# S5's state turned back on VectorE and GpSimd before the read-out, and the scale of x moved to the context's stage

## The chip, the cores and the metric

The kernel runs on one core of a Trainium2 chip. The time is device microseconds (us) of that core for one execution. TensorE does the matrix products, VectorE and ScalarE the element-wise work, GpSimd almost nothing, and SyncE's queue starts the DMA transfers.

## What is computed

Two blocks run one after the other on a sequence of 256 tokens of width 2048, in fp32. The first mixes an S5 branch and a gated delta-rule branch, and closes with a convolved feed-forward. The second modulates its input by vectors computed from a condition, then runs windowed attention beside a two-way RWKV recurrence over a context of 256 tokens and over x, then a feed-forward. Cut to what the change touches:

```
# S5, 64 groups of 16 channels, 64 complex states each
_, _, xr, xi = lax.associative_scan(combine, (ar_t, ai_t, bu_re, bu_im), axis=1)
y = (jnp.einsum("ghp,blgp->blgh", c_re.astype(f32), xr)
     - jnp.einsum("ghp,blgp->blgh", c_im.astype(f32), xi))
...
mod = jax.nn.silu(c) @ ada_w + ada_b                    # 2048 -> 6 x 2048
sh1, sc1, g1, sh2, sc2, g2 = jnp.split(mod[:, None, :], 6, axis=-1)
...
z  = modulate(rmsnorm_2(x,  norm1_g), sh1,  sc1)  @ w_in     # x * (1 + scale) + shift
zc = modulate(rmsnorm_2(xc, norm1_g), sh1c, sc1c) @ w_in
...
x = x + g1 * (jnp.concatenate([attn, rw], axis=-1) @ w_out)
x = x + g2 * swiglu(modulate(rmsnorm_2(x, norm2_g), sh2, sc2), ffn_w1, ffn_w3, ffn_w2)
```

## The kernel before

Data lies feature by feature: a tile is 128 features by 256 tokens. A scheduler (`tile.TileContext` with a timeline of its own) fixes the order of the instructions on every engine when the program is built; on the chip each engine works through its own list in order, and so does each DMA queue.

**Dense products** (`dense`, from L273). A weight is loaded in pieces of 256 by 512 (SyncE's queue), copied to a rounded high part on ScalarE (L269), and the low part is formed by a subtraction on VectorE (L270, called the weight split below). TensorE then does three products a piece (L298, L299, L301).

**The ada vectors.** The modulation is 2048 x 12288 weights, read once in 384 tiles of 128x512, and it is spread over the whole program. `ada_tick` takes one tile out of the list `self.ada`. `dense` calls it `tick_rate` times a weight piece: 0.72 at first, 0.2 in the context's path, 0.55 in the context's quads and the first feed-forward, 0.43 in the part of x, 0.5 in the second feed-forward. `ada_rows(n0, n1)` does 4 x (n1 - n0) tiles for the features n0 to n1 (in units of 128): for each quarter TensorE first spreads a piece of the condition over the partitions (`ada_c`, L235, a PSUM bank with the tag "ada" and one buffer), then each tile is loaded by SyncE's queue (L184, three buffers) and multiplied and summed by one VectorE instruction (L242). At the end two VectorE instructions write `mod` (L246, L247). Rows 0 to 16 are the shift of x, 16 to 32 its scale, 32 to 48 the gate, 48 to 64 and 64 to 80 the shift and scale of the second feed-forward, 80 to 96 its gate. `ada_start` sets the list for the first block, `ada_next` sets the one for the second when the first block is nearly through (after `w_out1`), and `ada_end` empties whatever is left of the list at once. `program` calls `ada_end` before `attention`.

**S5** (`s5_setup` from L826, `s5` from L912). The recurrence runs in a turning frame: two products bring the input into the states, VectorE turns them by cosine and sine, two scans run per state half, and VectorE multiplies the result V (real part V[0], imaginary part V[1]) by the cosine (P1) and the sine (P2). That gives four arrays of 128x256. The turned-back state is (P1[0] - P2[1], P1[1] + P2[0]); the read-out takes the four arrays separately, with the matrices CP[0], CP[1] = -CP[0], CN and CN, and lets PSUM add them (L958 to L960). 64 groups in pairs make 32 rounds of this, in 16 pairs of rounds.

**Attention** (`attention` from L1634). For each of 4 key heads and 2 query blocks: scores (L1667, L1670), softmax, transposes (L1683), the output products (`at_po`, L1689), and a spread of the sums' reciprocals into the same tile (L1702). The tile of `at_po` has the PSUM tag "ada" too, with one buffer. The scheduler lays the RWKV quads of x beside it: scores (L1352), a block inversion (L627 to L642) and a chain of four steps (L1433 to L1462) for each quad.

Of the kernel before, what the change touches and what calls it, by code (L numbers as in the profile page):

```python
# [14 lines left out]
ALU = mybir.AluOpType  # L15
# [74 lines left out]
class Kern:  # L90
# [87 lines left out]
    def ada_start(self):  # L178

        self.ada = itertools.chain(self.ada_rows(16, 32, 1), self.ada_cols(), self.ada_rows(16, 32))  # L180
# [37 lines left out]
    def ada_next(self):  # L218
        self.ada_end()
        self.ada = itertools.chain(self.ada_rows(32, 64), self.ada_rows(64, 80))  # L220
# [605 lines left out]
    def s5_setup(self):  # L826
        nc = self.nc
        v = nc.vector
# [40 lines left out]
        kr, ki = t("kr"), t("ki")  # L869
# [9 lines left out]
        cT = [self.tq([128, 32, 32], name=f"s5_c{w}") for w in range(2)]  # L879
        for w in range(2):  # L880
            nc.sync.dma_start(cT[w], self.a["s5_cT"][:, w])
        CP = [self.tq([128, 32, 32], name=f"s5_cp{w}") for w in range(2)]
        CN = self.tq([128, 32, 32], name="s5_cn")
        tm = self.tq([128, 32, 32], name="s5_ct")
        bk = lambda ap: ap.unsqueeze(2).to_broadcast([128, 32, 32])
        v.tensor_tensor(tm, cT[1], bk(ki), ALU.mult)
        v.tensor_tensor(CP[0], cT[0], bk(kr), ALU.mult)
        v.tensor_tensor(CP[1], tm, CP[0], ALU.subtract)
        v.tensor_tensor(CP[0], CP[0], tm, ALU.subtract)
# [22 lines left out]
    def s5(self):  # L912
# [6 lines left out]
        for i8 in range(8):  # L919
# [3 lines left out]
            for q0 in (0, 2):  # L923
# [18 lines left out]
                for e in range(2):  # L942
# [14 lines left out]
                    Q.append((P1[:, 0], P2[:, 1], P1[:, 1], P2[:, 0]))  # L957
                for k, C in enumerate((self.CP[0], self.CP[1], self.CN, self.CN)):  # L958
                    for e in range(2):
                        nc.tensor.matmul(py[rows[e]], lhsT=C[:, i + e], rhs=Q[e][k], start=k == 0, stop=k == 3)  # L960
# [216 lines left out]
    def mod1(self):  # L1177

        self.gs1 = self.tiny([128, 2, 16], name="gs1")
        for w in range(2):  # L1180
            self.nc.vector.scalar_tensor_tensor(self.gs1[:, w], self.mod[:, w, 16:32], 1.0, self.P("norm1_g"), ALU.add,
                                                ALU.mult)

        fw = self.P("final_norm_w")
        self.gfw, self.w2e = self.tiny([128, 16], name="gfw"), self.tiny([128, 16], name="w2e")
        self.nc.vector.tensor_tensor(self.gfw, self.gs1[:, 0], fw, ALU.mult)
        self.nc.vector.tensor_tensor(self.w2e, fw, fw, ALU.mult)
        self.nc.vector.tensor_scalar(self.w2e, self.w2e, EPS, None, ALU.add)
# [596 lines left out]
    def program(self, out):  # L1785
# [24 lines left out]
        self.tick_rate = 0.43  # L1810
        self.mid_norms()
# [122 lines left out]
```

## Time and profile before

| what | value |
|---|---|
| runs | 3480.36, 3486.3 and 3485.99 us, median 3485.99 |
| the profiled execution: its own time, its span | 3484.27 us, 3482.5 us |
| mean granted clock of TensorE | 0.975 of full speed |
| busy: TensorE, VectorE, ScalarE, GpSimd | 96%, 72%, 44%, under 1% |
| S5 beside dense products | 383 to 731 us |
| the 64 tiles of the scale of x | 592 to 893 us |
| second block's first 192 ada tiles | 893 to 2327 us |
| attention beside RWKV quads | 2345 to 2524 us |

The busy share is an average over stages with different limits. A stretch shows its own limit: the engine that is busy nearly all of the stretch sets the pace there. Where no engine is, they wait for each other, and the waits tell which step ends last. The granted clock says at which of its two levels TensorE ran.

### The profile page before, as it was taken

What the parts mean: (1) busy time and instruction counts of PE and PEld (TensorE: products, weight loads), DVE (VectorE), ACT (ScalarE), POOL (GpSimd) and SP (SyncE); (2) the same over time, 40 slices, a digit from 0 to 9 for tenths busy, and PEclk for the clock granted to TensorE, in tenths of its full rate; (3) what the DMA queues carried; (4) which work ended last, traced back from release to release, by engine and by line L of the source; (5) the groups of instructions that cost most, each with busy time, mean ns of one, the idle gap of its engine ahead of it and who ended that gap; (6) DMA issues with size and microseconds to landing.
All of it is one profiled execution on the core that took longest, in us unless ns stands there. A gap on an engine that the chain in (4) does not pass through costs nothing. (4 is left out here: it accounts for less than half of the span.)

```text
span 3482.5 us, 72752 instructions
## 1 busy us (share of the span) xinstructions
PE 3341.5 (96%) x30680; PEld 3073.5 (88%) x30680; DVE 2506.8 (72%) x4245; ACT 1515.8 (44%) x2148; POOL 17.0 (0%) x46
## 2 busy tenths in 40 slices
PE   8999999999999999999999999998898999999998
PEld 7889767898998889999999988886686999999997
DVE  7787777877668878967777778686666666665556
ACT  5434334444454444434444454443433443333433
POOL 0000000000000000000000000000000000000000
PEclk9999999999998999999999999997899999999999
DMA  7655555667654445456676664450123676655554
GB/s 234 184 167 172 179 173 183 190 217 254 209 176 158 139 160 165 157 192 225 227 230 219 223 198 148 141 174 2 33 98 100 211 226 225 228 188 182 182 187 146
DMA packets 337287, 618.37 MB, mean 178 GB/s; under 512 B 25184, under 2 KB 49504, under 8 KB 336960
## 3 DMA queue, kind: packets, MB, share of 16 engines
q1 hardware_dynamic: 336736, 612.66, 54.7%
q8 instruction: 240, 3.93, 0.5%
q0 software_dynamic: 224, 1.07, 0.1%
q14 instruction: 87, 0.71, 0.1%
HBM read 608.39 MB, written 4.72 MB: 176 GB/s over the span
## 5 line engine op out<-in xcount | busy, mean ns | idle before, releaser
L270 DVE TENSOR_TENSOR wl<-w,wr 128x1024 fp32r<-128x1024 f32 (+2 forms) x928 | 1110.5, 1197 | 654.2 <-ACT wr L269 619.8
L269 ACT CAST wr<-w 128x1024 fp32r<-128x1024 f32 (+2 forms) x928 | 953.3, 1028 | 1382.6 <-PE acc L299 1172.0
L298 PE MATMUL acc<-hh,wr 128*128 128x256 f32 (+2 forms) x4976 | 1255.1, 287 | 35.0 <-DVE conv L378 10.3
L299 PE MATMUL acc<-hl,wr 128*128 128x256 f32 (+2 forms) x4976 | 1247.8, 286 | 5.1 <-DVE hl L317 3.2
L298 PEld LDWEIGHTS acc<-hh,wr 128*128 128x128 f32 (+2 forms) x4976 | 957.7, 193 | 75.5 <-issue 31.3
L299 PEld LDWEIGHTS acc<-hl,wr 128*128 128x128 f32 (+2 forms) x4976 | 958.6, 193 | 22.7 <-issue 16.4
L301 PE MATMUL acc<-hh,wl 128*128 128x256 f32 (+2 forms) x4976 | 749.6, 286 | 6.5 <-DVE wl L270 6.4
L301 PEld LDWEIGHTS acc<-hh,wl 128*128 128x128 f32 (+2 forms) x4976 | 660.5, 193 | 30.9 <-DVE wl L270 10.9
L298 PE MATMUL acc<-hid,wr 128*128 128x256 f32 x1408 | 355.6, 286 | 3.1 <-DVE x L1128 3.0
L299 PE MATMUL acc<-hid,wr 128*128 128x256 f32 x1408 | 353.3, 284 | 0.0
L298 PEld LDWEIGHTS acc<-hid,wr 128*128 128x128 f32 x1408 | 270.2, 192 | 7.2 <-DVE x L1128 3.7
L299 PEld LDWEIGHTS acc<-hid,wr 128*128 128x128 f32 x1408 | 270.3, 192 | 1.5 <-issue 1.1
L242 DVE SCALAR_TENSOR_TENSOR w_ada<-w_ada,ada_c 128x512 f32<-128x512 f32 x384 | 260.2, 679 | 3.8 <-PE ada_c L235 3.3
L301 PE MATMUL acc<-hid,wl 128*128 128x256 f32 x1408 | 223.9, 285 | 1.5 <-DVE wl L270 1.5
L301 PEld LDWEIGHTS acc<-hid,wl 128*128 128x128 f32 x1408 | 191.9, 192 | 4.4 <-DVE wl L270 1.9
L1107 DVE SCALAR_TENSOR_TENSOR fconv<-acc,pv,fconv 128x255 f32<-128x255 f32 (+1 forms) x176 | 81.2, 477 | 16.5 <-ACT fconv L1105 14.7
L298 PE MATMUL acc<-mrgh,wr 128*128 128x256 f32 x256 | 65.1, 289 | 2.9 <-ACT wr L269 2.9
L299 PE MATMUL acc<-ys5l,wr 128*128 128x256 f32 x256 | 64.3, 287 | 2.3 <-DVE ys5l L317 2.3
L298 PE MATMUL acc<-ys5h,wr 128*128 128x256 f32 x256 | 64.1, 287 | 1.1 <-ACT ys5h L316 1.0
L1352 PE MATMUL rw_ps<-rw_AR,rw_BK 64*128 64x64 f32 (+1 forms) x512 | 61.0, 294 | 4.0 <-ACT rw_BKT L1359 2.4
L299 PE MATMUL acc<-mrgl,wr 128*128 128x256 f32 x256 | 64.4, 287 | 0.0
L1105 ACT ACTIVATE fconv<-acc,pv 128x256 f32<-128x256 f32 x88 | 40.4, 471 | 53.2 <-PE acc L301 27.7
(537 smaller groups left out, 3733.2 us busy)
## 6 DMA issues: line engine op xcount, KB each, us to landing
w<-in_w_dram SPq DMA_DIRECT2D x264, 512.0 KB, 3.6
w<-in_w_in_dram SPq DMA_DIRECT2D x256, 512.0 KB, 4.0
w_ada<-in_ada_wT_dram SPq DMA_DIRECT2D x384, 256.0 KB, 4.2
w<-in_ffn_up_dram SPq DMA_DIRECT2D x176, 512.0 KB, 4.1
w<-in_ffn_down_dram SPq DMA_DIRECT2D x88, 512.0 KB, 4.1
w<-in_w_out_dram SPq DMA_DIRECT2D x64, 512.0 KB, 4.3
w_ada<-in_ada_w_dram SPq DMA_DIRECT2D x64, 256.0 KB, 2.7
w<-in_glu_w_dram SPq DMA_DIRECT2D x32, 512.0 KB, 4.2
```

What stands on the lines that cost most here:

```text
L242: nc.vector.scalar_tensor_tensor(w, w, 1.0, ps, ALU.mult, ALU.mult, accum_out=self.part[:, n - n0, q:q + 1])
L269: nc.scalar.copy(r[:, :kb, :w], t[:, :kb, :w])
L270: self.wsub = nc.vector.tensor_tensor(l[:, :kb, :w], t[:, :kb, :w], r[:, :kb, :w].bitcast(F32), ALU.subtract)
L298: nc.tensor.matmul(o, lhsT=a, rhs=xh(kt), start=kt == 0 and first_j, stop=False)
L299: nc.tensor.matmul(o, lhsT=a, rhs=xl(kt), start=False, stop=False)
L301: nc.tensor.matmul(o, lhsT=a, rhs=xh(kt), start=False, stop=kt == KT - 1 and last_j)
L1105: nc.scalar.activation(t[:, j], ps[:, j], AF.Copy, scale=w(2))
L1107: v.scalar_tensor_tensor(t[:, j, k:], ps[:, j, :256 - k], w(2 - k), t[:, j, k:], ALU.mult, ALU.add)
L1352: nc.tensor.matmul(pss[e][:, c], lhsT=bk(d, c)[hs[e]], rhs=AR[hs[e], d, :, cs], start=True, stop=True)
```

## The change

Three things are done. (1) In `s5`, one VectorE subtraction forms P1[0] - P2[1] in place and one GpSimd addition forms P1[1] + P2[0] in place; the read-out is then two products a round, with CP and CN, where it was four. (2) CP[1] is not built any more in `s5_setup`. (3) The tiles for the scale of x (`ada_rows(16, 32)`, 64 tiles) leave the list of the first block and become the first entry of the list of the second; `mod1` is split, and the part that needs the scale of x is called after `ffn1`. The rates of the ticks are as they were.

```diff
     def ada_start(self):
-        self.ada = itertools.chain(self.ada_rows(16, 32, 1), self.ada_cols(), self.ada_rows(16, 32))
+        self.ada = itertools.chain(self.ada_rows(16, 32, 1), self.ada_cols())
...
     def ada_next(self):
         self.ada_end()
-        self.ada = itertools.chain(self.ada_rows(32, 64), self.ada_rows(64, 80))
+        self.ada = itertools.chain(self.ada_rows(16, 32), self.ada_rows(32, 64), self.ada_rows(64, 80))
...
-        CP = [self.tq([128, 32, 32], name=f"s5_cp{w}") for w in range(2)]
+        CP = self.tq([128, 32, 32], name="s5_cp")
...
-        v.tensor_tensor(CP[0], cT[0], bk(kr), ALU.mult)
-        v.tensor_tensor(CP[1], tm, CP[0], ALU.subtract)
-        v.tensor_tensor(CP[0], CP[0], tm, ALU.subtract)
+        v.tensor_tensor(CP, cT[0], bk(kr), ALU.mult)
+        v.tensor_tensor(CP, CP, tm, ALU.subtract)
...
                     v.tensor_tensor(P1, V, cb, ALU.mult)
                     v.tensor_tensor(P2, V, sb, ALU.mult)
-                    Q.append((P1[:, 0], P2[:, 1], P1[:, 1], P2[:, 0]))
-                for k, C in enumerate((self.CP[0], self.CP[1], self.CN, self.CN)):
+                    v.tensor_tensor(P1[:, 0], P1[:, 0], P2[:, 1], ALU.subtract)
+                    nc.gpsimd.tensor_tensor(P1[:, 1], P1[:, 1], P2[:, 0], ALU.add)
+                    Q.append(P1)
+                for k, C in enumerate((self.CP, self.CN)):
                     for e in range(2):
-                        nc.tensor.matmul(py[rows[e]], lhsT=C[:, i + e], rhs=Q[e][k], start=k == 0, stop=k == 3)
+                        nc.tensor.matmul(py[rows[e]], lhsT=C[:, i + e], rhs=Q[e][:, k], start=k == 0, stop=k == 1)
...
     def mod1(self):
-        for w in range(2):
-            self.nc.vector.scalar_tensor_tensor(self.gs1[:, w], self.mod[:, w, 16:32], 1.0, self.P("norm1_g"), ALU.add,
-                                                ALU.mult)
+        self.mod1_of(1)
+    def mod1_of(self, w):
+        self.nc.vector.scalar_tensor_tensor(self.gs1[:, w], self.mod[:, w, 16:32], 1.0, self.P("norm1_g"), ALU.add,
+                                            ALU.mult)
+    def mod1_x(self):
+        self.mod1_of(0)
...
         self.ffn1()
         self.tick_rate = 0.43
+        self.mod1_x()
```

Three places show how the order of the instructions moves.

TensorE in S5, the read-out of one pair of rounds, before (s_py is the read-out's bank, s_p the turned arrays, s_cp and s_cn the read-out matrices; acc are dense products, L940 brings the next input in):

```order
L940 MATMUL s_pw<-s_u_3337,s_b 128x256 x4
L298 MATMUL acc_5058<-ydnh_3862,wr 128x256
L299 MATMUL acc_5058<-ydnl_3864,wr 128x256
L298 MATMUL acc_5058<-ydnh_3862,wr 128x256
L301 MATMUL acc_5057<-ydnh_3862,wl 128x256 x4
L299 MATMUL acc_5058<-ydnl_3864,wr 128x256
L298 MATMUL acc_5058<-ydnh_3862,wr 128x256
L960 MATMUL s_py<-s_p_4092,s_cp_4035 32x256
L960 MATMUL s_py<-s_p_4082,s_cp_4036 32x256
L960 MATMUL s_py<-s_p_4092,s_cp_4036 32x256
L960 MATMUL s_py<-s_p_4082,s_cn 32x256
L960 MATMUL s_py<-s_p_4092,s_cn 32x256
```

The same place in the changed kernel:

```order
L301 MATMUL acc_5055<-ydnh_3862,wl 128x256 x4
L301 MATMUL acc_5056<-ydnh_3862,wl 128x256 x3
L961 MATMUL s_py<-s_p_4080,s_cp 32x256
L939 MATMUL s_pw<-s_u_3337,s_b 128x256 x4
L301 MATMUL acc_5056<-ydnh_3862,wl 128x256
L201 MATMUL ada_ps<-w_ada,pv 32x512
L301 MATMUL acc_5191<-hh_156,wl 128x256 x4
L298 MATMUL acc_5191<-hh_156,wr 128x256
L299 MATMUL acc_5191<-hl_160,wr 128x256
L961 MATMUL s_py<-s_p_4092,s_cp 32x256
L961 MATMUL s_py<-s_p_4080,s_cn 32x256
L961 MATMUL s_py<-s_p_4092,s_cn 32x256
```

The pair's first product (before, one row above these) and the seven that follow become four; the two that read CP come first, the two with CN, which read GpSimd's half, come last, and the last of the pair stand together as before.

VectorE between the last weight splits of the part of x and the attention, before (L242 is an ada tile, L246 and L247 write `mod`, L1601 and L1602 are the rotary step):

```order
L242 SCALAR_TENSOR_TENSOR w_ada,part<-w_ada,ada_c 128x512
L270 TENSOR_TENSOR wl<-w,wr 128x1024 x2
L242 SCALAR_TENSOR_TENSOR w_ada,part<-w_ada,ada_c 128x512
L246 TENSOR_REDUCE mod<-part 128x16
L247 TENSOR_TENSOR mod<-mod,pv 128x16
L1734 SCALAR_TENSOR_TENSOR gs_30583<-mod,pv 128x16
L270 TENSOR_TENSOR wl<-w,wr 128x1024 x3
L1601 TENSOR_TENSOR rope_t<-rope_ps,rope 128x512
L1602 TENSOR_TENSOR rope_raw<-rope_raw,rope 128x512
L1297 SCALAR_TENSOR_TENSOR rw_kk<-xk_24777,pv,rw_pk 128x256
```

The same place in the changed kernel:

```order
L242 SCALAR_TENSOR_TENSOR w_ada,part<-w_ada,ada_c 128x512
L246 TENSOR_REDUCE mod<-part 128x32
L247 TENSOR_TENSOR mod<-mod,pv 128x32
L270 TENSOR_TENSOR wl<-w,wr 128x1024 x3
L242 SCALAR_TENSOR_TENSOR w_ada,part<-w_ada,ada_c 128x512 x3
L1606 TENSOR_TENSOR rope_t<-rope_ps,rope 128x512
L1607 TENSOR_TENSOR rope_raw<-rope_raw,rope 128x512
L1302 SCALAR_TENSOR_TENSOR rw_kk<-xk_24566,pv,rw_pk 128x256
L1608 TENSOR_TENSOR x_kv_26092<-rope_raw,rope_t 128x512
L242 SCALAR_TENSOR_TENSOR w_ada,part<-w_ada,ada_c 128x512
```

Before, the list of ada tiles is through with three weight splits still to come; now only rows up to 64 are through by then (the reduction writes 32 columns), and the 64 tiles of rows 64 to 80 follow behind the last weight split, among the attention's first instructions.

TensorE where the attention's first output products stand, before (at_ps are scores, at_pt transposes, inv an RWKV block inversion):

```order
L1683 MATMUL at_pt<-cst,at_p 128x128 x4
L635 MATMUL inv_27781<-invDT,invB_27779 32x16 x23
L1683 MATMUL at_pt<-cst,at_p 128x128 x4
L1667 MATMUL at_ps<-at_ks,at_qs 128x512 x2
L1670 LDWEIGHTS at_mi
L1670 MATMUL at_ps<-at_mi 128x128
L635 MATMUL inv_27781<-invDT,invB_27779 32x16 x12
L1689 MATMUL at_po<-at_PT,vt 64x128 x8
```

The rows ahead of the first output products in the changed kernel (L235 is ada_c, the last quarter of the 64 tiles; rw_ are RWKV products of a quad):

```order
L235 MATMUL ada_c<-cst,pv 128x128 x4
L1438 MATMUL rw_px<-rw_S,rw_AR 64x64 x8
L1446 MATMUL rw_py<-rw_AR,rw_S 64x64 x8
L1450 MATMUL rw_pa<-rw_X,invDT_27709 64x64 x8
L1357 MATMUL rw_ps<-rw_AR,rw_BK 128x128 x8
L1467 MATMUL rw_py<-rw_M_27429,rw_SAV_27552 64x64 x4
L1467 MATMUL rw_py<-rw_M_27471,rw_SAV_27552 64x64 x4
L1363 MATMUL rw_pt<-cst,rw_BK 128x128 x4
L1357 MATMUL rw_ps<-rw_AR,rw_BK 128x128 x8
L1363 MATMUL rw_pt<-cst,rw_BK 128x128 x4
L1357 MATMUL rw_ps<-rw_AR,rw_BK 128x128 x8
L1363 MATMUL rw_pt<-cst,rw_BK 128x128 x4
```

The first output products, which before stood among one quad's inversion steps, now stand behind the last ada_c, behind that quad's chain of steps and behind the next quad's scores, two rows below these (L1694, 16 instructions); the list of SyncE's queue has the loads of the 64 tiles ahead of the attention's key loads and of those of x (`x3_load`).

## Rows read from the trace of the kernel before

**Rows 1.** The page: span, and busy us, share and instructions of each engine

```profile
span 3482.5 us, 72752 instructions
PE 3341.5 (96%) x30680; PEld 3073.5 (88%) x30680; DVE 2506.8 (72%) x4245; ACT 1515.8 (44%) x2148; POOL 17.0 (0%) x46
```

**Rows 2.** Stretches: length; busy PE, PEld, DVE, ACT, POOL; clock, DMA share, GB/s

```profile
383.00:700.00 317.00, 316.58 (x2137) 239.63 (x2136) 249.41 (x409) 130.47 (x149) 0.00 (x0) 1.00 0.57 182
592.00:893.00 301.00, 293.00 (x2298) 271.67 (x2297) 242.33 (x424) 144.65 (x191) 0.00 (x0) 0.98 0.68 221
893.00:2327.00 1434.00, 1388.97 (x13581) 1318.20 (x13580) 1097.32 (x1886) 651.81 (x950) 10.12 (x26) 0.98 0.57 184
2345.00:2364.00 19.00, 6.41 (x93) 4.54 (x95) 18.57 (x39) 10.53 (x24) 0.00 (x0) 0.56 0.00 1
2364.00:2524.00 160.00, 141.64 (x1857) 104.05 (x1855) 98.73 (x233) 62.31 (x159) 2.96 (x8) 0.82 0.06 19
2524.00:2638.00 114.00, 105.33 (x1317) 85.65 (x1318) 72.22 (x131) 41.82 (x70) 1.03 (x2) 0.94 0.22 75
```

**Rows 3.** Stretch table of line 960 alone: length, busy PE and PEld

```profile
383.00:731.00 348.00, 41.69 (x256) 14.95 (x256) 1.00 0.57 183
```

**Rows 4.** Timeline of TensorE in S5: start us, length us, instructions

```profile
424.67 1.03 PE L960 MATMUL s_py<-s_p,s_cn 128*32 128x256 f32 x6
425.53 1.02 PE L201 MATMUL ada_ps<-w_ada,pv 128*32 128x512 f32 x2
```

**Rows 5.** Groups by line and form: count, busy us, mean ns, idle before

```profile
L949 DVE TENSOR_TENSOR s_p<-s_p 128x256 f32<-128x256 f32 x32 | 13.3, 416 | 0.0
L578 POOL MEMSET invR<- 128x256 f32 x9 | 3.0, 331 | 873.4 <-DVE rw_ta L1322 250.9 <-DVE hl L317 216.4 <-DVE rw_el L1316 144.8
L242 DVE SCALAR_TENSOR_TENSOR w_ada<-w_ada,ada_c 128x512 f32<-128x512 f32 x384 | 260.2, 679 | 3.8 <-PE ada_c L235 3.3
L242 DVE DVE_READ_ACCUMULATOR w_ada<-w_ada,ada_c 128x1 f32 x384 | 31.3, 81 | 0.0
```

**Rows 6.** Stretch table of line 242 alone; two entries for each tile

```profile
592.00:731.00 139.00, 19.02 (x56) 0.99 0.61 193
592.00:893.00 301.00, 43.65 (x128) 0.98 0.68 221
893.00:2327.00 1434.00, 131.98 (x384) 0.98 0.57 184
```

**Rows 7.** Loads of ada tiles, line 184, issued from 400 to 600 us

```profile
DMA to landing us min/median/max: 2.3/2.7/5.1
```

**Rows 8.** Timeline of VectorE ahead of the attention

```profile
2333.69 1.23 DVE L270 TENSOR_TENSOR wl<-w,wr 128x1024 fp32r<-128x1024 f32 x1 [2.13 <-ACT wr L269]
2366.75 0.48 DVE L637 SCALAR_TENSOR_TENSOR invDT<-inv,cst,invDT 128x256 f32<-128x256 f32 x1
```

**Rows 9.** Timeline of TensorE in the attention and behind it

```profile
2363.41 1.57 PE L1689 MATMUL at_po<-at_PT,vt 128*64 128x128 f32 x16
...
2397.18 0.71 PE L1702 MATMUL at_po<-at_rs,cst 4*128 4x128 f32 x4
...
2406.47 0.68 PE L1433 MATMUL rw_px<-rw_S,rw_AR 64*64 64x64 f32 x16
...
2412.45 0.71 PE L1702 MATMUL at_po<-at_rs,cst 4*128 4x128 f32 x4
...
2437.04 0.71 PE L1702 MATMUL at_po<-at_rs,cst 4*128 4x128 f32 x4
...
2523.29 0.71 PE L1702 MATMUL at_po<-at_rs,cst 4*128 4x128 f32 x4
...
2564.96 1.14 PE L627 MATMUL inv<-invD,rw_N 32*32 32x32 f32 x111
```

**Rows 10.** Groups on TensorE from 2524 to 2566 us

```profile
L1352 PE MATMUL rw_ps<-rw_AR,rw_BK 64*128 64x128 f32 x48 | 5.8, 285 | 0.0
L1358 PE MATMUL rw_pt<-cst,rw_BK 128*128 128x128 f32 x16 | 2.5, 279 | 0.0
```

## The prediction

> **What bounds the kernel now.** I read the page first, for the busy shares: TensorE is busy 3341.5 of 3482.5 us and GpSimd all but idle [rows 1]. An average over stages says little, so next the table of stretches [rows 2]. In 383 to 700 us, where S5 runs beside dense products, TensorE is busy 316.58 of 317 us and VectorE 249.41: TensorE alone sets the pace, and work taken from it there shortens the run one for one. In 592 to 893 us TensorE lacks only 8 us. In 2364 to 2524 us, the attention, it looks busy (141.64 of 160), but its mean granted clock is 0.82 of full, so much of that lies at the lower level of 1.2 GHz; the 19 us before show 6.41 us of TensorE against 18.57 of VectorE. There the bound changes hands: TensorE, VectorE and ScalarE pass work round, and no large product fills the gaps. DMA moves 19 GB/s there and 221 in 592 to 893.
>
> **The change part by part.** Sums are made against the profiled execution: 3484.27 us, with its span of 3482.5 and 1.8 around it. The median of the runs is 3485.99, 1.7 more, so the forecast is the same to 0.05%.
>
> *Read-out products.* 128 products become 64. All of them occupy TensorE for 41.69 us [rows 3], so half is 20.8; from start to start six of their instructions took 0.86 us [rows 4], 0.143 each, and 128 of the 256 instructions make 18.4. I take 20. It lies on the path, because TensorE had no gap there.
>
> *Sums on VectorE and GpSimd.* 32 sums of 128x256 come to VectorE at 416 ns [rows 5]: 13.3 us. From the same stage go 28 of the moved ada products (56 entries in 592 to 731, 19.02 us) [rows 6], so VectorE loses load and TensorE still hides it: nothing. One subtraction of 128x1024 in the setup falls away, off the path: nothing. If that cover went (the read-out waits for the sum), rival 3 prices it. GpSimd gets 32 sums, which the trace does not show. Its nearest row is a memset of the same shape, 331 ns, which only writes; with two operands read as slowly as that one writes it would be 0.99 us. Taken: about 0.8, 26 us of GpSimd in a stage of 348 us, beside other work. GpSimd's first sum of a pair runs while VectorE still works on the second state, and TensorE's order puts the products that read GpSimd's half last, so I charge nothing and keep 0 to 20 us for the range.
> The Trainium skill, GPSIMD Engine Reference, section "Performance versus the Vector engine", gives a two-input sum on GpSimd 1.96 times VectorE's time; by that one sum would take an estimated 0.82 us, and the sum above stays as it is. Its section "Key points" says that GpSimd contends with VectorE instructions that have two SBUF inputs, which speaks against the change; no run here shows it yet.
>
> *The 64 ada tiles leave 592 to 893 us.* 43.65 us of VectorE [rows 6] and 64 loads go. TensorE's idle time there, 8 us, bounds the gain from above, 0 from below; the moved work was seldom what it waited for. Taken: 2.
>
> *The 64 tiles arrive.* The rates of the ticks are not changed. From 893 to 2327 us the kernel finishes 192 tiles (384 entries) [rows 6]; with 256 to do, it still gets 192 done, and the call that drains the list before the attention issues the last 64 in one go. The order shows exactly that: behind the last weight split VectorE has 64 ada products among the attention's first instructions. This hits the one place with nothing to hide it: the attention's output bank carries the same tag as the bank that holds the ada vector, one buffer, so the first attention output cannot start before the last of the 64 has been read. SP's queue has them too, in front of the attention's key loads (six of them) and of x3.
> How long they take: before, the weight split ends at 2333.69 + 1.23 = 2334.9 and VectorE works without a pause worth naming to its first inversion step at 2366.75 [rows 8]. The first 16 tiles stand among that work: 16 x 0.68 = 11 us more, 2378. For the other 48 there are two prices. By loads: three buffers, each turn a landing of 2.7 us (least 2.3) [rows 7] plus the product, 0.68 + 0.08 [rows 5], 3.5 us for three tiles, 1.15 each: 55. By VectorE in series: 48 x 0.68 = 33 plus the RWKV steps that stand between them, which before ran from 2366.75 to the fourth state product at 2406.47 [rows 8, 9], 40 us: 72. The queue is served in order, so a load that is late holds a chain step and the other way round; I take 65, nearer to the series. First attention output at 2443 instead of 2363.4 [rows 9]: 80 late (65 to 95).
> What TensorE does meanwhile: one RWKV quad's inversion and four steps, which before lay inside the attention. So the attention comes out shorter. Its eight blocks took 160 us, 20 each; the quickest block, with chain steps only, took 15.3 (2397.18 to 2412.45), one with inversion or score products 24.6 (2412.45 to 2437.04) [rows 9]. Now the first block is ready at once (6), three have light company (3 x 15) and four heavy (4 x 26): 155. The last output is 75 late.
> After it: the third quad's scores and first inversion products already lie behind it, which before came up to 2564.96, 41 us later [rows 9]. They occupy TensorE for 5.8 and 2.5 us [rows 10] and 1.14 [rows 9], 9.4 together, and most of the 9 us that TensorE idles in 2524 to 2638 [rows 2] should go, since the chain behind them starts earlier: 9 to 18. Taken: 17 back. The loss is 75 - 17 = 58.
> *The scale itself* is one small vector instruction, later by some 1400 us and long before it is read: nothing. It also moves later the shift and gate vectors of the second feed-forward; they are read behind the attention: nothing.
>
> **Sum.** -20 - 2 + 58 = +36: 3484.3 + 36 = 3520.
>
> **The rivals.** *1, faster: the burst is hidden.* DMA and VectorE have room (VectorE 98.73 of 160 us, DMA almost none) [rows 2]; were the path through the attention the RWKV chain and not the outputs, the 64 tiles would fill gaps only, and the attention would catch up. It decides if the first output is late by 18 us or less, since up to 18 are won back behind it. Time: 3484 - 20 = 3464. Against it stands the shared bank and that even back to back on VectorE the burst takes 64 x 0.68 = 44 us. *2, within 0.2%: half hidden.* The least case of the terms, 44 us late, 18 won back and 22 saved: 3488. *3, slower still: the read-out waits for GpSimd.* TensorE takes its queue in order, so each of the 16 pairs of groups can stand still for one sum of up to 0.99 us, 16 us, and VectorE, if it is held, delays weight splits behind it. S5's 20 us would be gone: 3540. For it: TensorE has no slack there and the sum is the last rung of its ladder; against: today's read-out stands a chunk of dense products behind its operand and never stalled. *4, slower still: the burst costs the upper ends,* 95 late and 9 back, or a TensorE that stays at its lower level after long gaps as in 2345 to 2364 (0.56) [rows 2]: 3484 - 22 + 86 to 90 = 3548 to 3552. *5, the change does not do what it says:* the scheduler spreads the 64 earlier. The order excludes it.
>
> **How the numbers follow.** Forecast 0.56 (3500 to 3538), rival 1 0.07, rival 2 0.08, rival 3 0.14, rival 4 0.15. Time: 3520. The range leaves out rival 1 and the upper half of rival 4, with what lies under 3490: 3490 to 3553. A measurement of this kernel tells 0.2%, 7 us, from no change: faster 0.07, same 0.08, slower 0.85.
>
> **What would show it.** Right: in 383 to 731 us the read-out products' own busy time halves to some 21 us, TensorE stays without gaps, and the stage ends about 20 us sooner; no ada product lies in 592 to 893, and 64 lie behind the last weight split at about one per 1.2 us; the first attention output starts 60 to 95 us behind the ada vector before it in shifted time; the attention then takes about 155 us. The GpSimd sum lasts 0.4 to 1 us. Wrong: a burst of some 45 us, an attention that starts within 40 us, or TensorE idling in S5 in front of the products that read the GpSimd half.

## The result, and the profile after

The changed kernel runs in 3517.67 us (median of 3514.3, 3516.5, 3518.84 and 3526.35), the kernel before in 3486.14 us (its three runs and one more of 3488.88). The ratio is 1.0094, 95% interval 1.0078 to 1.0111: 33 us slower, 27 to 39. The forecast was 3520 us. Runs of one kernel differ by some 10 us here, and a trace is one run. The profiled execution has a span of 3512.5 us, 30 more than before, and that difference is the one to be found in the traces.

The page of the changed kernel, busy time of each engine (to be read against [rows 1]):

```profile
span 3512.5 us, 72690 instructions
PE 3332.2 (95%) x30552; PEld 3074.3 (88%) x30552; DVE 2522.3 (72%) x4276; ACT 1515.2 (43%) x2149; POOL 110.7 (3%) x78
```

TensorE is busy for 9 us less and the run is 30 us longer, so TensorE idles about 39 us more. Where, shows in the starts of the same products in both kernels. Groups of the kernel before: behind the count, ns of one (least, median, most), then the start of the first and of the last in us (acc<-ys5h is the first dense product behind S5, called the gated product below, acc<-mrgh the one behind it, acc<-rwh the second half of the output product behind the attention):

```profile
L960 PE MATMUL s_py<-s_p,s_cn x128: 379/379/403, 404.4 to 729.2; 128*32 128x256 f32 x128
L298 PE MATMUL acc<-ys5h,wr x256: 278/283/415, 713.1 to 813.7; 128*128 128x256 f32 x128
L298 PE MATMUL acc<-mrgh,wr x256: 278/283/582, 814.5 to 921.2; 128*128 128x256 f32 x128
L1689 PE MATMUL at_po<-at_PT,vt x256: 272/273/476, 2363.4 to 2523.1; 128*64 128x128 f32 x128
L298 PE MATMUL acc<-rwh,wr x128: 277/283/582, 2636.9 to 2690.1; 128*128 128x256 f32 x128
```

The same groups of the changed kernel:

```profile
L961 PE MATMUL s_py<-s_p,s_cn x64: 379/379/636, 409.0 to 704.3; 128*32 128x256 f32 x64
L298 PE MATMUL acc<-ys5h,wr x256: 278/283/583, 685.0 to 788.1; 128*128 128x256 f32 x128
L298 PE MATMUL acc<-mrgh,wr x256: 278/283/387, 788.8 to 886.2; 128*128 128x256 f32 x128
L1694 PE MATMUL at_po<-at_PT,vt x256: 272/273/477, 2407.6 to 2557.1; 128*64 128x128 f32 x128
L298 PE MATMUL acc<-rwh,wr x128: 278/283/582, 2668.0 to 2720.0; 128*128 128x256 f32 x128
```

The gated product starts 28 us sooner (713.1 and 685.0), the next one 25.7 us sooner (814.5 and 788.8) and ends 35.0 us sooner (921.2 and 886.2). The attention's first output comes 44 us later in absolute time, and the second half of the output product 31.1 us later. So the first block won 35 us (36 by the last weight split), and the part from there to 2668 us lost 67. Both are larger than forecast (22 and 58), and the two misses cancel for the most part.

**The burst.** The stretch table of the changed kernel answers to the last three lines of [rows 2]; the columns are the same:

```profile
2298.00:2408.00 110.00, 65.92 (x886) 51.77 (x888) 88.41 (x233) 27.84 (x64) 1.48 (x4) 0.63 0.54 168
2408.00:2558.00 150.00, 130.99 (x1525) 96.26 (x1525) 98.22 (x233) 60.60 (x153) 2.52 (x6) 0.79 0.07 23
2558.00:2668.00 110.00, 94.23 (x1083) 74.08 (x1082) 56.06 (x91) 34.79 (x55) 0.00 (x0) 0.89 0.23 78
```

VectorE's timeline at its start, TensorE's at its end (start, length, instruction, in brackets the idle time before it):

```profile
2297.70 1.23 DVE L270 TENSOR_TENSOR wl<-w,wr 128x1024 fp32r<-128x1024 f32 x1 [2.13 <-ACT wr L269]
2298.84 0.68 DVE L242 SCALAR_TENSOR_TENSOR w_ada<-w_ada,ada_c 128x512 f32<-128x512 f32 x1
```

```profile
2407.61 3.68 PE L1694 MATMUL at_po<-at_PT,vt 128*64 128x128 f32 x32
```

From the end of the last weight split (2297.70 + 1.23 = 2298.93) to the first output it is 108.7 us; before it was 2363.41 - 2334.92 = 28.5 [rows 8, 9]. The stretch table of line 242 alone, with two entries a tile, shows that no ada tile is left in the stretch of the first block, that 192 tiles are done in the second as before, and that all 64 others stand in the burst:

```profile
560.00:865.00 305.00, 0.00 (x0) 0.99 0.55 173
865.00:2291.00 1426.00, 131.89 (x384) 0.99 0.58 184
2298.00:2408.00 110.00, 43.30 (x128) 0.63 0.54 168
```

VectorE is through with the last of them at 2399.88 us:

```profile
2399.80 0.08 DVE L242 DVE_READ_ACCUMULATOR w_ada<-w_ada,ada_c 128x1 f32 x1
```

So the burst lasts 101 us, 1.6 us a tile. The first output comes 7.7 us later, because TensorE's list has the next quad's scores ahead of it. The chain of waits (start, length, what) in the burst's second half alternates between a landing and the product it releases:

```profile
2365.26 3.09 DMA w_ada<-in_ada_wT_dram
2368.44 0.71 DVE w_ada L242 x2
2369.16 3.23 DMA w_ada<-in_ada_wT_dram
2372.49 0.70 DVE w_ada L242 x2
```

Each turn is a landing of some 3.1 us and a product of 0.7, 3.9 us for the three buffers. Over the whole chain from 2280 to 2420 us landings make up 25.5% and ada products 15.8%; the rest is the dense products ahead of the burst and steps of the RWKV chain and of the attention. TensorE meanwhile has one RWKV quad to do and its granted clock is 0.63.

### The profile page after: what moved, and what is told of

It reads as the page before. It is cut to its first block, busy times and chain, and to the rows that moved or that the text cites. A ratio compares the mean times of both kernels' runs of the same rounds, so it can differ in the third digit from the quotient of the medians.

```text
span 3512.5 us, 72690 instructions
## 1 busy us (share of the span) xinstructions
PE 3332.2 (95%) x30552; PEld 3074.3 (88%) x30552; DVE 2522.3 (72%) x4276; ACT 1515.2 (43%) x2149; POOL 110.7 (3%) x78
## 5 line engine op out<-in xcount | busy, mean ns | idle before, releaser
L242 DVE SCALAR_TENSOR_TENSOR w_ada<-w_ada,ada_c 128x512 f32<-128x512 f32 x384 | 259.8, 680 | 22.6 <-DMA w_ada<-in_ada_wT_dram 17.5
L957 POOL TENSOR_TENSOR s_p<-s_p 128x256 f32<-128x256 f32 x32 | 93.6, 2942 | 375.0 <-DVE s_p L955 349.1
L1357 PEld LDWEIGHTS rw_ps<-rw_AR,rw_BK 64*128 64x128 f32 x512 | 55.5, 212 | 14.6 <-issue 7.6
```

The lines of the kernel that those rows point to most:

```text
L242: nc.vector.scalar_tensor_tensor(w, w, 1.0, ps, ALU.mult, ALU.mult, accum_out=self.part[:, n - n0, q:q + 1])
L957: nc.gpsimd.tensor_tensor(P1[:, 1], P1[:, 1], P2[:, 0], ALU.add)
L1357: nc.tensor.matmul(pss[e][:, c], lhsT=bk(d, c)[hs[e]], rhs=AR[hs[e], d, :, cs], start=True, stop=True)
```

## The experiments

The changed kernel's edits are called the read-out (two products, two sums) and the move (64 tiles to the second block) here. Differences in us are worked out from the ratio to the kernel before, times 3486.

| run | ratio, 95% interval | us against before |
|---|---|---|
| changed kernel | 1.0094 (1.0078 to 1.0111) | +33 |
| read-out alone | 0.9970 (0.9959 to 0.9982) | -10 |
| move alone | 1.0161 (1.0146 to 1.0176) | +56 |
| move alone, no burst | 0.9965 (0.9949 to 0.9981) | -12 |
| both, sums on VectorE | 1.0105 (1.0085 to 1.0124) | +37 |
| both, products doubled | 1.0137 (1.0121 to 1.0153) | +48 |
| both, burst left out | 0.9902 (0.9874 to 0.9929) | -34 |
| both, no burst, late rate | 0.9902 (0.9877 to 0.9927) | -34 |
| both, no burst, all rates | 1.0004 (0.9986 to 1.0022) | +1 |
| both, half a burst | 0.9968 (0.9956 to 0.9980) | -11 |
| both, burst without loads | 1.0056 (1.0032 to 1.0080) | +20 |
| both, output tile in another bank | 1.0245 (1.0230 to 1.0260) | +85 |
| both, fewer tiles beside the context's quads | 0.9938 (0.9918 to 0.9958) | -22 |

### The read-out alone

```diff
-        self.ada = itertools.chain(self.ada_rows(16, 32, 1), self.ada_cols())
+        self.ada = itertools.chain(self.ada_rows(16, 32, 1), self.ada_cols(), self.ada_rows(16, 32))
...
-        self.ada = itertools.chain(self.ada_rows(16, 32), self.ada_rows(32, 64), self.ada_rows(64, 80))
+        self.ada = itertools.chain(self.ada_rows(32, 64), self.ada_rows(64, 80))
```

> The read-out part alone: two products and the two sums, the 64 tiles of the scale of x back in the first block. By the sum in the prediction the products are worth 20 us: 3466 us. By the trace of the changed kernel, which is 27 us ahead at the end of S5 and 35 us ahead at 920 us, it depends on whose gain that is. If all of it belongs to the read-out: 3451 us. If the last 8 us belong to the tiles that left: 3459 us. Rival: the sums only fit on VectorE and GpSimd because the tiles left that stage; then the gain is mostly gone, 3480 us, and TensorE waits for s_p in front of the read-out.

It runs in 3480.43 us, 10 us below before by the ratio: the rival's figure, and none of the other three. The profiled run is 10 us faster than that median (3470.57); it is 9 us ahead of before by 912 us, 5 by the last weight split, and the rest of its lead comes in the attention's stage. The same groups in its trace:

```profile
L961 PE MATMUL s_py<-s_p,s_cn x64: 379/379/636, 408.6 to 718.2; 128*32 128x256 f32 x64
L298 PE MATMUL acc<-ys5h,wr x256: 278/283/582, 684.2 to 805.2; 128*128 128x256 f32 x128
L298 PE MATMUL acc<-mrgh,wr x256: 274/283/581, 805.9 to 912.4; 128*128 128x256 f32 x128
```

TensorE reaches the gated product at 684.2 us, as early as in the changed kernel, but the last read-out of S5 comes at 718.2 us and not at 704.3, and the gated product needs 121.7 us and not 103.8 (684.2 to 805.9, 685.0 to 788.8). The waits of TensorE in 690 to 770 us (what waited, for what: total, times, longest) name VectorE most:

```profile
PE s_py L961 <- DVE s_p L956: 7.2, 1, 7.2
PE acc L301 <- DVE wl L270: 5.5, 2, 5.0
```

In 680 to 700 us VectorE is busy for 19.36 of 20 us and TensorE for 15.27; in 710 to 720 us TensorE is busy for 2.66 of 10 us at the lower clock level (0.50):

```profile
680.00:700.00 20.00, 15.27 (x104) 12.76 (x102) 19.36 (x37) 11.42 (x17) 5.42 (x3) 0.91 0.50 145
710.00:720.00 10.00, 2.66 (x8) 0.73 (x8) 6.97 (x15) 0.58 (x1) 2.99 (x2) 0.50 0.00 0
```

So TensorE finishes the dense work that covers S5 early, and then waits for VectorE's last rounds. With the 64 tiles still in that stage, VectorE ends it.

### The move alone, with the burst and without

The first is the kernel before with the tiles moved and S5 as it was. The second also raises the rate from the fifth slice of the first feed-forward on (the late slices below, where plain dense products run), so that the list is through before the attention:

```diff
         for s in range(nsl + 1):
+            if not acc_last and s == 4:
+                self.tick_rate = 0.92
```

> The move of the 64 tiles alone, with four products as before. By the prediction -2 and +58: 3542 us. By the trace of the changed kernel, whose attention part costs 65 us: -8 and +65 gives 3543 us if the tiles that leave give 8 us, 3551 us if they give nothing. Together with the read-out alone the differences to before should add up to the +31.5 us of the whole change to within 5 us; if not, the two parts help each other in S5's stage.

> The tiles' move with the late rate of 0.92, so without a burst, and with S5's four products as before: the fourth corner beside the kernel before, the read-out alone and the version with both. From the move alone less what the late rate gave to the changed kernel: 3543 - 63 = 3480 us. The read-out is then worth 25 us where the tiles have left S5's stage, against 9 where they stand in it. If the read-out is worth the same in both places, 3464 us.

They run in 3543.36 and 3472.28 us, +56 and -12. The read-out alone (-10) and the move alone without a burst (-12) add up to -22; both together, in the run with the late rate below, give -34. With the burst, -10 and +56 make +46, and the change measures +33. Either way the two parts are worth 12 to 13 us more together than apart, with some 10 us of noise on each such sum. The first block of the traces, where both act, says the same: the product behind the gated one ends at 921.2 us before, 912.4 with the read-out, 904.3 with the move and 886.2 with both, so 8.8 and 16.9 us apart, 35.0 together, 9 us more. The groups of the move without burst:

```profile
L960 PE MATMUL s_py<-s_p,s_cn x128: 378/379/404, 403.9 to 705.8; 128*32 128x256 f32 x128
L298 PE MATMUL acc<-ys5h,wr x256: 280/283/387, 714.0 to 805.8; 128*128 128x256 f32 x128
L298 PE MATMUL acc<-mrgh,wr x256: 278/283/387, 806.5 to 904.3; 128*128 128x256 f32 x128
```

Here it is the other way round: VectorE is through at 705.8 us, TensorE comes at 714.0 only, and the gated product runs through in 92.5 us without a wait. The stage's end is the later of two arrivals, and each part of the change brings forward one of them. The move relieves TensorE too, which the prediction leaves out: a quarter's condition is spread by TensorE (L235), and of 40 such products from 383 to 1000 us 8 are left, 4.8 us less (before, then the changed kernel; length, busy PE and PEld):

```profile
383.00:1000.00 617.00, 5.90 (x40) 5.20 (x40) 0.99 0.62 201
383.00:1000.00 617.00, 1.06 (x8) 0.97 (x8) 0.99 0.59 185
```

The gain of 9 us behind it belongs to the move: the next dense product runs from its first to its last in 97.8 us here and 97.4 in the changed kernel, against 106.7 before and 106.5 with the read-out alone.

### The sums on VectorE, and the products doubled

```diff
-                    nc.gpsimd.tensor_tensor(P1[:, 1], P1[:, 1], P2[:, 0], ALU.add)
+                    v.tensor_tensor(P1[:, 1], P1[:, 1], P2[:, 0], ALU.add)
```

> The changed kernel with GpSimd's 32 sums done by VectorE. In the changed kernel GpSimd needs 2.94 us for one (0.72 where VectorE rests), VectorE 0.42. If VectorE's load ends S5's stage, as the read-out alone suggests: 32 x 0.42 = 13 us later, 3531 us. If it has slack there: 3518 us. Rival: GpSimd's stretched sums hold the read-out at the stage's end, and VectorE's short ones make it 3 to 8 us faster, 3510 to 3515 us.

```diff
-                for k, C in enumerate((self.CP, self.CN)):
+                for k, C in enumerate((self.CP, self.CP, self.CN, self.CN)):
...
-                        nc.tensor.matmul(py[rows[e]], lhsT=C[:, i + e], rhs=Q[e][:, k], start=k == 0, stop=k == 1)
+                        nc.tensor.matmul(py[rows[e]], lhsT=C[:, i + e], rhs=Q[e][:, k // 2], start=k == 0, stop=k == 3)
```

> The changed kernel with each of the two read-out products issued twice, so 128 products again beside the sums (y of S5 comes out doubled in its state part). It prices the products alone. By the prediction's row 20 us: 3538 us. By the trace, in which the changed kernel gains 28 us by 670 us: 3546 us. Rival: VectorE, not TensorE, ends S5's stage once the products are halved; then the extra products are hidden in part and it stays under 3530 us.

With the sums on VectorE the run is 8 us longer by the medians (3525.47 and 3517.67), 4 by the ratios, whose intervals overlap, so the times alone do not show a cost. In the traces the last read-out moves from 704.3 to 710.4 us and the product behind the gated one from 788.8 to 796.8. That is VectorE's 13 us in part, and the direction agrees with a stage that VectorE ends; the rival, a gain, did not come.

The doubled products cost 15 us by the ratios (1.0137 and 1.0094, intervals apart), in the traces 22 us where the gated product starts (707.2 and 685.0) and 11 us where it ends. Their price on TensorE up to the gated product is near the forecast's 20; half of it is given back in that product, which runs through in 92.5 us here (707.2 to 799.7) and needs 103.8 in the changed kernel, where TensorE is there before VectorE's last rounds.

### The burst left out, and spread over the late slices

The first leaves the 64 tiles out, and with them the values that they compute (a memset, not shown, stands for these). The second is the changed kernel with the late rate shown above. The edit of the first:

```diff
-        self.ada = itertools.chain(self.ada_rows(16, 32), self.ada_rows(32, 64), self.ada_rows(64, 80))
+        self.ada = itertools.chain(self.ada_rows(16, 32), self.ada_rows(32, 64))
```

> The changed kernel without the last 64 tiles: the rows 64 to 80 of the modulation (shift and scale of the second feed-forward) are not computed, a memset stands for them. It prices the burst as a whole. By the two traces (from 36 ahead at 2250 us to 30 behind at the end): 3518 - 65 = 3453 us. If part of the loss belongs to the order of the RWKV quads and not to the burst, 3465 to 3490 us.

> The changed kernel with the rate 0.92 for 0.55 from the fifth slice of the first feed-forward on, so that the 64 tiles go into the stretch where dense products alone run (TensorE 98% busy, VectorE 73%, DMA 0.70 in the trace of before) and not beside the context's RWKV quads, where the raised rates lost 28 us. No burst is left. If the place decides: the 35 us of the first block stay and the 65 us of the burst go, 3450 to 3462 us. Rival: 64 tiles cost some 25 to 30 us in any stretch, through VectorE or the loads: 3480 us.

Both are at 0.9902: 3453.64 and 3455.43 us. So the burst costs 33 + 34 = 67 us, and beside plain dense products the same 64 tiles cost nothing that the times can tell from leaving them out, to within some 10 us. There the DMA share rises from 0.68 to 0.79 and VectorE from 344.78 to 373.90 of 470 us, and TensorE stays busy for 97% or more (the late slices, the kernel before and then the version with the late rate):

```profile
1500.00:1970.00 470.00, 460.69 (x3878) 456.41 (x3873) 344.78 (x538) 198.76 (x238) 1.05 (x2) 1.00 0.68 222
```

```profile
1500.00:1970.00 470.00, 457.72 (x3820) 453.68 (x3818) 373.90 (x641) 200.17 (x239) 1.05 (x2) 1.00 0.79 253
```

The traces show a small price in place all the same: in these 470 us TensorE gets 58 fewer products done (3820 for 3878), some 7 us. From the weight split that starts at 1506 us before to the one at 2292, it takes 785.8 us before, 785.6 in the changed kernel, 787.4 with the tiles left out and 794.9 with the late rate. This version is faster than both kernels.

### All rates raised by a third

```diff
-        self.tick_rate = 0.2
+        self.tick_rate = 0.27
...
-        self.tick_rate = 0.55
+        self.tick_rate = 0.74
...
-        self.tick_rate = 0.43
+        self.tick_rate = 0.58
```

> The changed kernel with the three tick rates of the second block raised by 256/192 (0.27, 0.74, 0.58 for 0.2, 0.55, 0.43), so that all 256 tiles are through by the last weight split and nothing is left to drain. If the loss is the burst alone: 3518 - 65 = 3453 us, and the first attention output comes about 30 us behind the last weight split, as before. Rival: 64 tiles more cost their VectorE time (64 x 0.68 = 44 us) or their loads wherever they stand: about 3490 us.

3487.08 us: the rival's figure. The burst is gone here too, but most of its gain is lost elsewhere. Same products compared, the profiled run (3492.66) is 32 us ahead of before at 1101 us and 4 us ahead at 1401 us: beside the context's RWKV quads. TensorE is busy 206.91 of 220 us in the later part:

```profile
1180.00:1400.00 220.00, 206.91 (x2511) 189.47 (x2510) 181.16 (x346) 95.39 (x154) 1.93 (x6) 0.95 0.49 152
```

The changed kernel, with the old rates, needs 190.5 us from the weight split that starts at 1177.2 us to the one at 1367.7, and TensorE is busy nearly all of it; the version with the late rate, whose order is the same up to there, needs 194.5, and with the raised rates it is 214.7:

```profile
1178.00:1370.00 192.00, 188.93 (x2427) 174.42 (x2427) 162.10 (x300) 91.78 (x149) 2.05 (x6) 0.99 0.50 162
```

That the reason is the tiles' place in VectorE's list, between the steps of a chain as in the burst, is argued and not shown. Nor is all of the 28 us the rates': by the weight split at 1425 us the changed kernel and the five versions below and above with the same order up to there are 19 to 30 us ahead, each in one run, and this one 1.5.

### Half a burst, a burst without loads

Half a burst is the late rate at 0.735 in place of 0.92, which leaves 32 tiles. The burst without loads multiplies the same three tiles over and over:

```diff
-            if i + 2 < len(steps):
+            if i + 2 < len(steps) and (n0 != 64 or i == 0):
                 ahead.append(load(*steps[i + 2]))
             w = ahead.pop(0)
+            if n0 == 64:
+                ahead.append(w)
```

> The version with the raised late rate, but at 0.735 in place of 0.92, so that about 32 of the 64 tiles are left for the burst ahead of the attention. If the burst costs about 1 us a tile: 3455 + 32 = 3487 us. If the attention gives back the first 18 us, as the prediction's second half has it: about 3470 us.

> The changed kernel with the burst's 64 products on VectorE but only three loads for them: the products read the same three tiles again, so the rows 64 to 80 of the modulation are wrong. In the trace of the changed kernel the burst takes 102 us, 1.6 us a tile, and VectorE waits 15 us in it for landings. If loads set its pace: 20 to 40 us of the loss go, 3478 to 3498 us. If VectorE's list in series with the RWKV chain sets it, as in the prediction's larger price: only the 15 us of waits go at most, 3503 to 3518 us.

Half a burst: 3476.38 us, 23 us above none and 44 below the whole. So the first 32 tiles cost 0.7 us each and the last 32 cost 1.4: neither of the two expectations, between them. That the attention gives back part of a short delay and little of a long one would fit; it was not traced further.

Without the loads the run is 3505.04 us, 13 less than the changed kernel (the intervals just touch), inside the second expectation, near the end that the waits for landings set. The first output comes 26 us sooner behind the last weight split (82.6 us against 108.7), and the second half of the output product 18 us sooner (351.1 against 369.0):

```profile
L1696 PE MATMUL at_po<-at_PT,vt x256: 272/273/476, 2387.2 to 2542.0; 128*64 128x128 f32 x128
L300 PE MATMUL acc<-rwh,wr x128: 278/283/582, 2655.8 to 2707.8; 128*128 128x256 f32 x128
```

The last tile is read here at 2387.14 us, and the first output starts at once (2387.19):

```profile
2387.06 0.08 DVE L244 DVE_READ_ACCUMULATOR w_ada<-w_ada,ada_c 128x1 f32 x1
```

So the burst takes 82.5 us for 101 with the loads: the landings make up under a fifth of it, and the rest is the products themselves between the other steps in VectorE's list. The other 8 of the 26 us are the scores that stand ahead of the first output in the changed kernel.

### The output tile in another bank

```diff
-                pob = self.ps.tile([128, 2, 256], F32, tag="ada", name="at_po", bufs=1)
+                pob = self.pm([128, 2, 256], name="at_po")
```

> The changed kernel with the attention's output tile taken from the four buffers of tag m instead of the one of tag ada; the burst of 64 tiles stays. If the shared bank is what holds the first output back, the outputs start while the burst runs, and most of the 65 us goes: 3465 to 3485 us. Rival: the burst holds the attention through the lists worked in order (ada_c in TensorE's list waits for 16 tiles read, the loads stand ahead of the key loads in SyncE's queue, the 64 products in VectorE's list); then the time stays within 15 us of 3518.

3574.02 us, slower still by 52 (by the ratios), which neither theory had. The bank did hold the first output back: it now starts at 2308.3 us, 26 us behind the last weight split (2282.3) and long before the burst ends. But the attention then runs beside the burst and alone behind it (its outputs end at 2436 us, the last tile at 2378), and the RWKV quads that were to run beside it follow without cover:

```profile
2436.00:2700.00 264.00, 201.24 (x2838) 161.02 (x2837) 176.39 (x366) 82.42 (x162) 4.45 (x12) 0.75 0.14 45
```

TensorE idles 63 us in it. From the last weight split to the second half of the output product it is 417.7 us, against 302.0 before, 369.0 in the changed kernel and 292.9 with the late rate. Of the 53 us between the two traces, 32 are lost by that product's start (2700.0 and 2668.0) and 21 in it: it runs for 72.8 us from first to last, 52.0 in the changed kernel. The reading that attention and RWKV quads cover each other's waits, and that the burst takes the place of one of them, fits the first part; what made the second was not looked for. The edit changes the scheduler's order as a whole, so it tells what the bank is worth only together with that order.

### Fewer tiles beside the context's quads

The edit to the version with the late rate: 1.02 in place of 0.92, and 0.35 in place of 0.55 before it.

> The version with the late rate, with tiles taken out of the first feed-forward's first four slices as well, where the context's RWKV quads run: rate 0.35 for 0.55 there (some 18 tiles fewer) and 1.02 for 0.92 after. With rates raised there by a third, the kernel had lost 28 us beside the quads. If a tile there costs what that says, over 1 us each: 3455 - 15 = 3440 us. If the tiles only move from one full stretch to another (DMA at 250 GB/s in the late slices): 3455 us, or slower by up to 10.

3466.87 us, -22 against the -34 of the version with the late rate: not faster. Same products compared, it is 7 us ahead of that version at 1540 us, but the changed kernel and the version with the burst left out, whose order is the same up to there, lie 12 us apart at that place (36 and 24 ahead of before), so a gain beside the quads is not shown. It is level at 2271 us, since the late slices take 802.3 us here for 794.9, and then it loses 6 us in the stage of the attention (298.6 and 292.9 us from the last weight split to the second half of the output product). Both run the same instructions there in an order that differs somewhat; what in the order costs the 6 us, and the rest of the difference between the medians, was not looked for.

## Why the prediction was right

The sign, the time and the main mechanism came out as forecast: 3517.67 for 3520 us, 64 tiles in one burst behind the last weight split, the attention held back by them. Two terms were off, by 13 us of gain and 9 of loss, and cancelled for the most part; that the time is met to 2 us is luck.

- **Read-out, -20.** The price of the products is about right: 22 us by the start of the gated product with the products doubled. The reason given for "one for one" was not: [rows 2] ended at 700 us, and the stage does not. Before, the last read-out at 729.2 us came behind the first gated product at 713.1, so VectorE's rounds already ended after TensorE had come to that product. Alone the read-out gives 10 us. Nor did TensorE stay without gaps in the changed kernel, as the prediction has it: it idles 5 us in 680 to 713 us. And the read-out's own busy time did not halve to the 21 us named as a sign ([rows 3]: 41.69 us; here line 961, length, busy PE and PEld):

```profile
383.00:731.00 348.00, 28.53 (x128) 8.21 (x128) 0.99 0.56 174
```

  A record lasts 379 ns in the median before and after; six side by side took 1.03 us [rows 4], and in the changed kernel more of them stand singly between other products, so this sum says little of what they cost.
- **The tiles leave, -2, and "VectorE loses load: nothing".** This is the step that failed. The tiles' place in S5 was costed at nothing because TensorE set the pace; it is worth 8 us at S5's end (814.5 to 806.5 us where the gated product ends, in the move without burst), and 9 more by the traces with the read-out. The 8 us are not VectorE's time alone: TensorE's waits and its lower clock in 713 to 730 us (0.90, then 1.00) go, and 16 of the 32 products of L235. The stretch behind gave 9 us, where 2 of at most 8 were taken; the bound of 8 counted TensorE's idle time and not the other 16 products of L235 (2.4 us) nor the clock there (0.97, then 1.00). First block: -35 for -22.
- **GpSimd's sum, 0.8 us.** Wrong by a factor of more than three: 2.94 us on average, 7.79 at most. It cost nothing all the same. TensorE's products waited for a GpSimd sum for 0.7 us in all of S5 (its weight loads for 1.8), and rival 3 has no support: the stage ended sooner.
- **First attention output 80 us late.** Measured 108.7 - 28.5 = 80.2. The sum behind it (11 + 65 us on top of the old 32) makes 108 us for 64 tiles, 1.7 each; the 1.2 named as a sign counts the delay alone. Measured: 101 us for the tiles, 1.6 each, and 7.7 for the scores ahead of the first output, which the sum does not have. The larger of the two prices, in series with the RWKV steps, was the nearer one, and the landings, 3.2 us in the median for 2.7 [rows 7], come on top:

```profile
DMA to landing us min/median/max: 2.8/3.2/5.1
```

- **The attention itself, 155 us.** Its outputs run for 150.4 us from the first to the end of the last, for 160.6 before: 10 won, 5 forecast.
- **17 us back behind it.** Only 3 came: from the last output to the second half of the output product it is 110.0 us, before 112.9. TensorE's busy time there fell by 11 us, from 105.33 to 94.23, but its waits in the norms of the RWKV output grew from 7 to 16 us (before 3.9 and 3.1 us for the same two lines):

```profile
PE rw_rs L425 <- DVE rw_nsq L417: 9.4, 4, 2.4
PE ns L406 <- ACT sq L1573: 6.4, 5, 2.0
```

  TensorE's work was not what that stage ended with. Loss of the part: 80 - 10 - 3 = 67 for 58.
- **The shared bank as the cause.** It holds the first output back, as told: without the loads the output starts with the last tile's end, and with another bank long before it. That the loss is the bank's is not shown: without it the loss was larger. What the runs show is that the burst costs 67 us ahead of the attention, and that the same tiles cost some 8 in the late slices.

What stays open: with the products doubled the first block was still 7 us ahead of the move with S5 as before (799.7 and 806.5 us where the gated product ends), although VectorE and GpSimd have more to do. The order differs; no run takes that apart.

## What to carry to other kernels

A stage that two engines share ends with the later of two arrivals: look at its last microseconds, not at its mean, and expect one edit to be worth less until the other engine's load goes too. Work that is spread by a rate must be counted again when the list grows; what the rate does not reach lands in one place, and here the drain stood where little covered it. Put filler beside long plain products: against leaving them out, the same 64 tiles cost nothing that the times can tell in the late slices (some 8 us in their place by the traces), 35 us with every rate raised and 67 us in one burst. And before a difference of 10 us inside one trace is given a cause, compare the same stretch in other runs whose order is the same there.

## What the runs showed of the hardware

GpSimd's addition of two 128x256 arrays in SBUF takes 0.72 us at the least and 2.94 on the average, and what stretches it is VectorE at work beside it. Of the 32 sums, the seven with no VectorE instruction beside them took 0.72 to 0.74 us. Of the twelve that took over 4 us, eleven had VectorE busy for all but some 0.6 us of their time, and one for all but 0.2. Line of the changed kernel (minimum, median, maximum in ns), then GpSimd's timeline at one pair of sums:

```profile
L957 POOL TENSOR_TENSOR s_p<-s_p x32: 717/1748/7792, 394.4 to 703.3; 128x256 f32<-128x256 f32 x32
```

```profile
417.93 6.22 POOL L957 TENSOR_TENSOR s_p<-s_p 128x256 f32<-128x256 f32 x2 [19.94 <-DVE s_p L955]
```

VectorE's timeline in the same microseconds:

```profile
417.70 1.22 DVE L270 TENSOR_TENSOR wl<-w,wr 128x1024 fp32r<-128x1024 f32 x1
...
419.17 0.68 DVE L954 TENSOR_TENSOR s_p<-s_v,s_r 128x512 f32<-128x512 f32 x1
419.77 0.68 DVE L955 TENSOR_TENSOR s_p<-s_v,s_f 128x512 f32<-128x512 f32 x1
420.38 0.42 DVE L956 TENSOR_TENSOR s_p<-s_p 128x256 f32<-128x256 f32 x1
420.71 1.22 DVE L270 TENSOR_TENSOR wl<-w,wr 128x1024 fp32r<-128x1024 f32 x1
421.85 0.68 DVE L930 TENSOR_TENSOR s_f<-s_f,s_r 128x512 f32<-128x512 f32 x1
422.45 0.42 DVE L956 TENSOR_TENSOR s_p<-s_p 128x256 f32<-128x256 f32 x1
424.88 1.23 DVE L270 TENSOR_TENSOR wl<-w,wr 128x1024 fp32r<-128x1024 f32 x1 [2.01 <-ACT s_r L932]
```

VectorE keeps its usual lengths (the weight split 1.2, the sum 0.42 us), and GpSimd's first sum, begun at 417.93, ends at 423.46, 0.6 us after VectorE's list has its first pause at 422.87; the second, with VectorE at rest, takes 0.73. The Trainium skill, GPSIMD Engine Reference, section "Key points", says that GpSimd shares its SBUF interfaces with VectorE and contends with VectorE instructions that have two SBUF inputs; the trace agrees, and adds that here nearly all of the waiting fell to GpSimd. Some short sums (0.75 us at 394.36) ran beside a busy VectorE as well, so which of its instructions hold GpSimd up stays open. The sums were not badly placed here, since TensorE hardly waited for them; a chain that had to wait for one would have paid up to 7.8 us.
